# A conv-and-pooling decoder step: pair one by the plain products, and first chunks of weights that bring two thirds of x

## The chip, the cores and the metric

The kernel runs on one core of a Trainium2 chip. The metric is device time in microseconds of one execution. Of the core's engines, TensorE (PE in the profile, PEld for its weight loads) multiplies, VectorE (DVE) and ScalarE (ACT) do the elementwise work, SyncE (SP) issues the DMAs, and GpSimd (POOL) does nearly nothing.

## The reference

One layer of a decoder on 1024 prompt tokens and 32 sample tokens, 1056 in all, of 1024 channels, in float32:

```python
h    = x * rsqrt(mean(x * x) + eps) * norm_g
proj = h @ w_in                      # 1024 -> 3072: b, c, u, z_a, v, z_b, 512 columns each
cu   = c * u
y_a  = b * conv3(cu) * silu(z_a)     # 3 taps over time
y_b  = ((window mean of v) - v) @ pool_w * pool_scale * silu(z_b)   # windows 2, 4, 8, 16
x    = x + concat(y_a, y_b) @ w_out
y    = x * rsqrt(mean(x * x) + eps) * final_g
```

The last rows of cu and v go out too, as new states.

## The kernel before

**Tokens and channels.** Channels lie on the 128 partitions: 1024 channels of x are 8 chunks k. The 1056 tokens are three thirds n = 0, 1, 2 of 352 columns. `raw[n]` holds a third of x as loaded. The factor of the first RMS norm is one number per token, and it is applied after the projection: `R` holds it for all tokens, `R2` its square.

**Precision.** A float32 operand is split into an upper and a lower half of a shorter type (`split`, `split2`: ScalarE writes the upper half on L154, VectorE the lower half on L155). A product is three matmuls: upper by lower, lower by upper, upper by upper.

**Pairs.** The 24 blocks of 128 output columns of `w_in` are done two at a time, 12 pairs (`PAIRS`). Pair 0 (`project_first`) is done plain: for each third of tokens, 8 chunks x 3 products x 2 outputs = 48 matmuls, as the chunks of weights (`wfraw`, L108) and of x (`raw`, L105) arrive. The first six issues of weights each come with the same chunks of third 2; thirds 0 and 1 follow in halves.

**Strassen pairs.** Pairs 1 to 11 treat thirds 0 and 1 as two rows of blocks, and the lower and upper 4 chunks as two columns: A11, A12 (third 0) and A21, A22 (third 1). With sums S1 to S4 of blocks of x and differences T1 to T4 of blocks of weights, seven block products of 12 matmuls do for eight (function `block`, L229). Third 2 (`pl`) is done plain. That is 7 x 12 + 2 x 24 = 132 matmuls a pair. The weights of a pair p are loaded (`load_w`, into `wraw`, one buffer), scaled by the norm's gain on ScalarE (`gain_w`, eight operations, L203), differenced on VectorE (`make_t`, L208 to L210) and split into four units a (B11, B21), b (B12, B22), c (T1, T3), d (T2, T4) (`make_unit`). Units have five buffers (tag "wt").

**Places.** Tiles with one tag share a place, or as many as the tag has buffers; a new tile of a full tag gets a place when an old one is given back. S1, S2, S3, S4 have the tags "xa", "xc", "xb", "xd"; "xa", "xc" and "xd" held `raw[2]`, `raw[1]`, `raw[0]`, and "xb" held A21. Before their splits, the float32 sums S1f, S3f, S2f are formed in place in `raw[1]` and `raw[0]` (L500, L501, L507), S4f in two buffers of its own. PSUM has eight banks, which go round.

**Sums of squares.** Rows of tokens 0 to 639 are squared on ScalarE with an accumulator (`square_rows`, tiles t = 0 to 4). The other tokens are squared by channel (`squares_head`, `squares_last`), added up on VectorE (`sums_head`, `sums_last`) into `acc`, and summed over the partitions by 8 small matmuls (`sums_rest`, L276). `rows` makes the reciprocal roots, in two halves on a diagonal (L285 to L299), and `rows_out` spreads them over partitions with 6 matmuls (L306) into R and R2.

**The order.** The first part, to the end of pair 1, stands in `tc.manual_schedule` for TensorE, ScalarE, VectorE and GpSimd: these engines take its instructions in the order in which they are written. From pair 2 on only TensorE's order is written by hand; a planner places the rest by its own costs. DMAs are placed by the planner throughout. Pair 2 runs through `strassen` with two hooks: `rest` (sums_rest and rows) after its third block, T1, and `rows` (rows_out) after the plain product "l".

Of the kernel before, what the change touches and what calls it, by code (L numbers as in the profile page):

```python
# [7 lines left out]
F32 = mybir.dt.float32  # L8
# [5 lines left out]
P = 128  # L14
D = 1024
KD = D // P
# [46 lines left out]
def trunk(ctx, tc, xt, xres, xct, w_first, w_in, w_out, pool_w, par, fg, sconv, spool,  # L63
# [40 lines left out]
    def load_x(n, k, m):  # L104
        nc.sync.dma_start(raw[n][:, k:k + m, :], xt[:, n * KD + k:n * KD + k + m, :])  # L105

    for k, m in ((0, 1), (1, 1), (2, 1), (3, 1), (4, 2), (6, 2)):
        nc.sync.dma_start(wfraw[:, k:k + m, :], w_first[:, k:k + m, :])  # L108
        load_x(2, k, m)
    for n in (0, 1):  # L110
        for k in (0, 4):
            load_x(n, k, 4)

    wraw = {}

# [50 lines left out]
    def split_x(n, k, m):  # L166
        dst = blocks[n, k // KH]
        ks = slice(k % KH, k % KH + m)
        split2(dst[:, 0, ks], dst[:, 1, ks], raw[n][:, k:k + m])
# [11 lines left out]
    pm = {}  # L181
# [53 lines left out]
    def load_rows(t, xk):  # L235
        nc.sync.dma_start(xk, xres[t * P:(t + 1) * P])
        return xk
# [7 lines left out]
    def squares_head(acc):  # L245
        sh = tmp("sq_h")[:, :KD * REST].rearrange("p (k c) -> p k c", k=KD)
        nc.scalar.activation(sh, raw[1][:, :, TN - REST:], AF.Square)
        return sh
# [160 lines left out]
    def strassen(p, S1, S2, S3, S4, hooks):  # L409
        (q, j), (_, _) = PAIRS[p]  # L410
        if q == "v":
            left = vb[:, PM:]
            right = szb[j] = tmp(f"szb_{j}")
            scale = R
        elif q == "c":
            left, right = tmp(f"t_{j}"), tmp(f"um_{j}")
            scale = R2
        else:
            left, right = tmp(f"z_{j}"), tmp(f"y_{j}")
            scale = R  # L420
        n0, n1, n2 = cols

        def plain(i, name):
            pt = bank(name)[:, :TN]
            block(pt, p, ("B11", "B12")[i], pl[0], True, False)
            block(pt, p, ("B21", "B22")[i], pl[1], False, True)
            return pt

        a = bank(f"a_{p}")[:, :TN]
        s1 = snap(f"s1_{p}")  # L430
        block(a, p, "B11", A11, True, False)
        nc.scalar.copy(s1, a)
        b = bank(f"b_{p}")[:, :TN]
        block(b, p, "T2", S2, True, False)
        t1 = snap(f"t1_{p}")
        vt(t1, b, s1, op=ADD)  # L436
        c = bank(f"c_{p}")[:, :TN]
        block(c, p, "T1", S1, True, False)
        hooks.get("rest", lambda: None)()
        pL = plain(0, f"l_{p}")  # L440
        hooks.get("rows", lambda: None)()
        vt(left[:, n2], pL, scale[:, n2], op=MUL)
        block(a, p, "B21", A12, False, True)
        vt(left[:, n0], a, scale[:, n0], op=MUL)
        block(b, p, "T3", S3, False, False)
        t2 = snap(f"t2_{p}")
        vt(t2, b, s1, op=ADD)
        vt(right[:, n1], c, t2, op=ADD)
        hooks["early"]()
        pR = plain(1, f"r_{p}")  # L450
        if q == "v":
            vt(right[:, n2], pR, R[:, n2], op=MUL)
        elif q == "c":
            vt(up[:, 2 + 2 * TN:], pR, left[:, n2], op=MUL)
        else:
            nc.scalar.copy(right[:, n2], pR)
        hooks["middle"]()
        block(b, p, "T4", A22, False, True)
        vt(left[:, n1], b, s1, op=ADD)
        vt(left[:, n1], left[:, n1], scale[:, n1], op=MUL)  # L460
        block(c, p, "B22", S4, False, True)
        vt(right[:, n0], c, t1, op=ADD)
        hooks["late"]()

        if q == "v":
            after_v(j)
            vt(right[:, both], right[:, both], R[:, both], op=MUL)
            silu(right)
        elif q == "c":
            vt(up[:, 2:2 + 2 * TN], right[:, both], left[:, both], op=MUL)  # L470
            after_u(j)
        else:
            silu(left)
            vt(left, left, keep["yc"], op=MUL)
            vt(right, right, left, op=MUL)
            finish_mix(right, f"a_{j}")
# [5 lines left out]
    with tc.manual_schedule(engines={ET.PE, ET.Activation, ET.DVE, ET.Pool}):  # L482
        for k in range(KD):
            prep_w0(k)
            split_x(2, k, 1)
            project_first(2, k)
        nc.vector.tensor_copy(gain.rearrange("p (k o) -> p k o", o=1), wfraw[:, :, 2 * P:])
        load_w(1)
        nc.sync.dma_start(part, par)
        xk = [load_rows(t, q[:, :D]) for t, q in enumerate((R, R2, up[:, 2:]))]  # L490
        acc = tmp("acc")
        for n in (0, 1):
            for k in range(0, KD, 2):
                split_x(n, k, 2)
            for k in range(KD):
                project_first(n, k)
        sh = squares_head(acc)

        S1f, S3f, S2f = raw[1][:, KH:], raw[1][:, :KH], raw[0][:, :KH]
        vt(S1f, raw[1][:, :KH], raw[1][:, KH:], op=ADD)  # L500
        vt(S3f, raw[0][:, :KH], raw[1][:, :KH], op=ALU.subtract)  # L501
        gain_w(1)
        make_unit(1, "a")
        for i in range(2):
            nc.scalar.copy(heads[i][:, n2], pm[i, 2])
        sq = squares_last()
        vt(S2f, S1f, raw[0][:, :KH], op=ALU.subtract)  # L507
        make_t(1)
        make_unit(1, "b")
        load_w(2)  # L510
        S4f = [tp.tile([P, 2, TN], F32, tag="tmp", name=f"S4f_{h}") for h in range(2)]
        for h in range(2):
            vt(S4f[h], raw[0][:, KH + 2 * h:KH + 2 * h + 2], S2f[:, 2 * h:2 * h + 2], op=ALU.subtract)
        S1 = xtile("xa", "S1")
        split(S1, S1f)
        make_unit(1, "c")
        S3 = xtile("xb", "S3")
        split(S3, S3f)
        x34 = wp.tile([P, 2, D], F32, tag="wt", bufs=5, name="x34")
        xk += [load_rows(t, x34[:, t - 3]) for t in (3, 4)]  # L520
        for t in range(3):
            square_rows(t, xk[t])
        for n in (0, 1):
            for i in range(2):
                nc.scalar.copy(heads[i][:, cols[n]], pm[i, n])


        t_0, um = tmp("t_0"), tmp("um_0")

        def plain1(i):  # L530
            pt = bank(f"lr{i}_1")[:, :TN]
            block(pt, 1, ("B11", "B12")[i], pl[0], True, False)
            block(pt, 1, ("B21", "B22")[i], pl[1], False, True)
            return pt

        pL = plain1(0)
        pa, pb, pc = (bank(f"{q}_1")[:, :TN] for q in "abc")
        s1, t1, t2 = (snap(f"{q}_1") for q in ("s1", "t1", "t2"))
        block(pa, 1, "B11", A11, True, False)
        nc.scalar.copy(s1, pa)  # L540
        pR = plain1(1)
        block(pa, 1, "B21", A12, False, True)
        S2 = xtile("xc", "S2")
        split(S2, S2f)
        make_unit(1, "d")
        S4 = xtile("xd", "S4")
        for h in range(2):
            ks = slice(2 * h, 2 * h + 2)
            split2(S4[:, 0, ks], S4[:, 1, ks], S4f[h])
        nc.scalar.copy(t_0[:, n2], pL)  # L550
        block(pb, 1, "T2", S2, True, False)
        vt(t1, pb, s1, op=ADD)
        block(pc, 1, "T1", S1, True, False)
        sums = sums_last(acc, sq)
        gain_w(2)
        make_unit(2, "a")
        nc.scalar.copy(t_0[:, n0], pa)
        next(sums)
        block(pb, 1, "T3", S3, False, False)
        vt(t2, pb, s1, op=ADD)  # L560
        vt(um[:, n1], pc, t2, op=ADD)
        make_t(2)
        for t in (3, 4):
            square_rows(t, xk[t])
        vt(up[:, 2 + 2 * TN:], pR, t_0[:, n2], op=MUL)
        make_unit(2, "d")
        block(pb, 1, "T4", A22, False, True)
        vt(t_0[:, n1], pb, s1, op=ADD)
        block(pc, 1, "B22", S4, False, True)
        vt(um[:, n0], pc, t1, op=ADD)  # L570
        make_unit(2, "c")
        sums_head(acc, sh)
        for _ in sums:
            pass
        make_unit(2, "b")
        vt(up[:, 2:2 + 2 * TN], um[:, both], t_0[:, both], op=MUL)
    diag = []
    nc.sync.dma_start(scb[:, :, 0:2 * NB], sconv)
    nc.sync.dma_start(spb[:, :, 0:15 * NB], spool)

    def scale_heads():
# [7 lines left out]
        nc.sync.dma_start(pwraw, pool_w)  # L589
        split(pws, pwraw)  # L590
        after_v(0)

    def rest():
        sums_rest(acc)
        diag.extend(rows())

    def rows_2():
        rows_out(diag)

    def pair(p):  # L600
        nxt = p + 1 < NP
# [18 lines left out]

        hooks = {"early": early, "middle": middle, "late": late}
        if p == 2:
            hooks.update(rest=rest, rows=rows_2)
        strassen(p, S1, S2, S3, S4, hooks)
        if p == 3:
            pool_linear(0)
# [218 lines left out]
```

## Time and profile before

| | |
|---|---|
| median of 3 runs | 378.48 us (378.38 to 378.67) |
| profiled execution, own time | 378.59 us |
| its span | 376.8 us |
| granted TensorE clock, mean | 0.999 |
| TensorE busy with matmuls | 365.3 us, 2114 matmuls |
| VectorE busy | 275.3 us |
| ScalarE busy | 177.5 us |
| DMA | 41.68 MB, mean 111 GB/s |
| chain that ended last | PE 80%, ACT 8%, DVE 5%, DMA 4% |

The own time is that of the whole execution; the span is what the trace covers, and all times of rows count from its start. A row of the order in time gives start, duration, engine, line, operation, the tiles (written <- read), the count of merged instructions, and in brackets how long the engine had been idle before and what released it. Matmuls overlap: a merged row of n matmuls ends some 0.16 us after the step of the last one. DMA rows give the size and the time from issue to landing.

### The profile page before, as it was taken

The numbers are of one execution on the slowest core, as the hardware profiler recorded it, in microseconds if no ns is written. First come the engines' busy times: TensorE is split into PE (matmuls) and PEld (weight loads), VectorE is DVE, ScalarE is ACT, GpSimd is POOL, SyncE is SP. The second block draws the span as 40 slices with busy tenths as digits, with TensorE's granted clock in tenths as the row PEclk, the third lists the DMA queues.
The fourth block names the chain that finished last, engine by engine and source line by source line (L and its number), as shares of the span: only waits on it lengthen the run. The fifth ranks groups of instructions, "written<-read, shape, count | busy, mean of one in ns | idle before, by whom it ended". The sixth has DMA issues, their size and how long they took to land.

```text
span 376.8 us, 5274 instructions
## 1 busy us (share of the span) xinstructions
PE 365.3 (97%) x2114; PEld 349.2 (93%) x2114; DVE 275.3 (73%) x420; ACT 177.5 (47%) x310; POOL 1.4 (0%) x7
## 2 busy tenths in 40 slices
PE   7999999999999999999999999999999999999993
PEld 4999978999999999999999999999988889999883
DVE  4889689899999977578898557788279537222593
ACT  5899952985343454537353352731078224111212
POOL 0000000000000000000000000000000000000000
PEclk9999999999999999999999999999999999999999
DMA  7975002104031312103040320404549913000042
GB/s 198 413 282 202 14 0 87 54 2 151 18 113 58 117 54 90 82 2 111 2 169 0 110 90 16 153 6 164 236 128 354 417 71 150 20 1 2 0 181 111
DMA packets 13368, 41.68 MB, mean 111 GB/s; under 512 B 3744, under 2 KB 4896, under 8 KB 11936
## 3 DMA queue, kind: packets, MB, share of 16 engines
q1 hardware_dynamic: 13200, 41.02, 29.6%
q8 instruction: 16, 0.26, 0.3%
q10 hardware_dynamic: 144, 0.33, 0.2%
q14 instruction: 8, 0.07, 0.0%
HBM read 32.92 MB, written 8.42 MB: 110 GB/s over the span
## 4 chain that ended last, share of the span: by engine, by line
PE 80%; ACT 8%; DVE 5%; DMA 4%; issue 1%; SPq 1%; DVEq 0%; ACTq 0%
PE b L229 15%; PE po L675 15%; PE r L229 10%; PE a L229 10%; PE c L229 10%; PE pc L745 10%; PE l L229 9%; DMA raw<-in_xt_dram 4%; ACT wraw L203 2%; PE pp L383 2%; ACT S L154 1%; ACT diag L298 1%; ACT sq L259 1%; ACT R L240 1%; DVE A L155 0%
## 5 line engine op out<-in xcount | busy, mean ns | idle before, releaser
L675 PE MATMUL po<-wo,mix 128*128 128x512 f32 (+1 forms) x264 | 56.5, 374 | 0.0
L675 PEld LDWEIGHTS po<-wo,mix 128*128 128x128 f32 x264 | 46.2, 188 | 9.7 <-DVE mix L155 0.2
L229 PE MATMUL a<-A,wa 128*128 128x352 f32 x264 | 46.5, 324 | 0.2 <-DVE wa L155 0.2
L203 ACT ACTIVATE wraw<-wraw,gain 128x256 f32<-128x256 f32 x88 | 36.9, 497 | 18.0 <-DMA wraw<-in_w_in_dram 17.4
L229 PEld LDWEIGHTS a<-A,wa 128*128 128x128 f32 x264 | 43.3, 188 | 0.5 <-DVE wa L155 0.5
L229 PE MATMUL l<-pl,wa 128*128 128x352 f32 x240 | 40.5, 324 | 0.0
L229 PE MATMUL r<-pl,wb 128*128 128x352 f32 x240 | 40.4, 324 | 0.0
L229 PEld LDWEIGHTS r<-pl,wb 128*128 128x128 f32 x240 | 39.1, 188 | 0.0
L229 PEld LDWEIGHTS l<-pl,wa 128*128 128x128 f32 x240 | 39.1, 188 | 0.0
L745 PE MATMUL pc<-mix,wo 128*128 128x416 f32 x192 | 36.5, 351 | 0.0
L745 PEld LDWEIGHTS pc<-mix,wo 128*128 128x128 f32 x192 | 35.9, 188 | 0.5
L154 ACT ACTIVATE wd<-tw 128x1024 fp32r<-128x1024 f32 x11 | 11.7, 1064 | 30.5 <-DVE tw L210 26.8
L229 PE MATMUL b<-S,wd 128*128 128x352 f32 x132 | 23.8, 326 | 1.2 <-DVE wd L155 1.1
L229 PE MATMUL b<-A,wd 128*128 128x352 f32 x132 | 23.2, 324 | 0.5 <-DVE t L560 0.5
L229 PEld LDWEIGHTS b<-S,wd 128*128 128x128 f32 x132 | 21.6, 188 | 2.0 <-DVE wd L155 1.7
L229 PE MATMUL b<-S,wc 128*128 128x352 f32 x132 | 23.2, 324 | 0.0
L229 PE MATMUL c<-S,wc 128*128 128x352 f32 x132 | 23.2, 324 | 0.0
L229 PE MATMUL c<-S,wb 128*128 128x352 f32 x132 | 23.1, 324 | 0.0
L229 PEld LDWEIGHTS b<-A,wd 128*128 128x128 f32 x132 | 21.6, 188 | 0.8 <-DVE t L560 0.8
L229 PEld LDWEIGHTS b<-S,wc 128*128 128x128 f32 x132 | 21.6, 188 | 0.2 <-DVE t L436 0.2
L229 PEld LDWEIGHTS c<-S,wc 128*128 128x128 f32 x132 | 21.6, 188 | 0.1
L229 PEld LDWEIGHTS c<-S,wb 128*128 128x128 f32 x132 | 21.7, 188 | 0.0
(196 smaller groups left out, 523.4 us busy)
## 6 DMA issues: line engine op xcount, KB each, us to landing
wraw<-in_w_in_dram SPq DMA_DIRECT2D x11, 1024.0 KB, 4.6
woraw<-in_w_out_dram SPq DMA_DIRECT2D x8, 512.0 KB, 5.9
raw<-in_xt_dram SPq DMA_DIRECT2D x4, 704.0 KB, 9.0
zt<-in_xres_dram SPq DMA_DIRECT2D x5, 512.0 KB, 6.5
spill_b<-yb SPq DMA_DIRECT2D x4, 528.0 KB, 3.0
mixraw<-spill_b SPq DMA_DIRECT2D x4, 528.0 KB, 6.7
out_yt_dram<-zt SPq DMA_DIRECT2D x4, 512.0 KB, 2.6
zc<-in_xct_dram SPq DMA_DIRECT2D x4, 416.0 KB, 6.7
```

The source lines that it names most:

```text
L154: nc.scalar.activation(hi, src, AF.Copy)
L203: nc.scalar.activation(t, t, AF.Copy, scale=gain[:, k:k + 1])
L229: nc.tensor.matmul(pt, t[:, a, i, k * P:(k + 1) * P], x[:, b, k], start=first and s == 0, stop=last and s == len(seq) - 1, skip_group_chec ...
L240: nc.scalar.activation(xk, xk, AF.Square, accum_out=ss[:, t:t + 1])
L259: nc.scalar.activation(t, raw[2][:, k:min(k + 3, KD)], AF.Square)
L298: nc.scalar.activation(dh[:, t * P:t * P + m], ident[:, :m], AF.Copy, scale=rh[:, t:t + 1].bitcast(F32))
L383: nc.tensor.matmul(pt[:, :TN], pws[:, a, g, :], pooled[g][b][:, cols[n]], start=(s == 0), stop=(s == 2))
L675: nc.tensor.matmul(pt, mix[k][:, b, t * P:(t + 1) * P], wo[k][:, a, c], start=(k == 0 and s == 0), stop=(k == KD - 1 and s == 2))
L745: nc.tensor.matmul(pt, wo[k][:, a, d * P:(d + 1) * P], mix[k][:, b, T0:], start=(k == 0 and s == 0), stop=(k == KD - 1 and s == 2))
```

## The change

Three things are changed.

- *Loads and pair 0.* The first chunks of weights come in five issues (1, 1, 2, 2, 2 chunks) instead of six, and each comes with the same chunks of third 2 and of third 0. Pair 0 is done chunk by chunk for thirds 2 and 0, then for third 1.
- *Pair 1.* Instead of the Strassen form it is done plain: for each third (2, 0, 1) two products of 24 matmuls, with units a and b only, into six banks `pq`. S1 and S3 are formed and split ahead of these products in the text, S2 and S4 after the first two. The copies of pair 0's banks for thirds 2 and 0 come ahead of them. The scaling, the differences and units of pair 2, the squares and sums follow in a new order.
- *Row sums.* `sums_rest` and `rows` stand at the end of the first part, ahead of pair 2 and in the order written; `rows_out` stands where `sums_rest` stood. Unit b of pair 2 comes after `rows`.

```diff
-    for k, m in ((0, 1), (1, 1), (2, 1), (3, 1), (4, 2), (6, 2)):
+    for k, m in ((0, 1), (1, 1), (2, 2), (4, 2), (6, 2)):
         nc.sync.dma_start(wfraw[:, k:k + m, :], w_first[:, k:k + m, :])
         load_x(2, k, m)
-    for n in (0, 1):
-        for k in (0, 4):
-            load_x(n, k, 4)
+        load_x(0, k, m)
+    for k in (0, 4):
+        load_x(1, k, 4)
...
         block(c, p, "T1", S1, True, False)
-        hooks.get("rest", lambda: None)()
+        hooks.get("rows", lambda: None)()
         pL = plain(0, f"l_{p}")
-        hooks.get("rows", lambda: None)()
...
             prep_w0(k)
-            split_x(2, k, 1)
-            project_first(2, k)
+            for n in (2, 0):
+                split_x(n, k, 1)
+                project_first(n, k)
...
+        for k in range(0, KD, 2):
+            split_x(1, k, 2)
+        for k in range(KD):
+            project_first(1, k)
         sh = squares_head(acc)
+        gain_w(1)
+        make_unit(1, "a")
+        make_unit(1, "b")
+        load_w(2)
+        for n in (2, 0):
+            for i in range(2):
+                nc.scalar.copy(heads[i][:, cols[n]], pm[i, n])
+        sq = squares_last()
+        square_rows(2, xk[2])
...
         S1 = xtile("xa", "S1")
         split(S1, S1f)
-        make_unit(1, "c")
         S3 = xtile("xb", "S3")
         split(S3, S3f)
...
+        for i in range(2):
+            nc.scalar.copy(heads[i][:, n1], pm[i, 1])
+        t_0 = tmp("t_0")
+        pq = {}
+        for n in (2, 0, 1):
             for i in range(2):
+                pt = pq[i, n] = bank(f"pq_{i}_{n}")[:, :TN]
+                for h in range(2):
+                    block(pt, 1, (("B11", "B21"), ("B12", "B22"))[i][h], blocks[n, h], h == 0, h == 1)
+        nc.scalar.copy(t_0[:, n2], pq[0, 2])
+        vt(up[:, 2 + 2 * TN:], pq[1, 2], t_0[:, n2], op=MUL)
         S2 = xtile("xc", "S2")
         split(S2, S2f)
         S4 = xtile("xd", "S4")
         for h in range(2):
             ks = slice(2 * h, 2 * h + 2)
             split2(S4[:, 0, ks], S4[:, 1, ks], S4f[h])
+        gain_w(2)
+        make_t(2)
+        make_unit(2, "a")
+        make_unit(2, "d")
+        x34 = wp.tile([P, 2, D], F32, tag="wt", bufs=5, name="x34")
+        xk += [load_rows(t, x34[:, t - 3]) for t in (3, 4)]
+        for t in range(2):
+            square_rows(t, xk[t])
+        nc.scalar.copy(t_0[:, n0], pq[0, 0])
+        vt(up[:, 2:2 + TN], pq[1, 0], t_0[:, n0], op=MUL)
         sums = sums_last(acc, sq)
         next(sums)
+        for t in range(3, 5):
             square_rows(t, xk[t])
         make_unit(2, "c")
+        nc.scalar.copy(t_0[:, n1], pq[0, 1])
+        vt(up[:, 2 + TN:2 + 2 * TN], pq[1, 1], t_0[:, n1], op=MUL)
         sums_head(acc, sh)
         for _ in sums:
             pass
+        sums_rest(acc)
+        diag = rows()
         make_unit(2, "b")
...
         if p == 2:
-            hooks.update(rest=rest, rows=rows_2)
+            hooks["rows"] = lambda: rows_out(diag)
```

`blocks[n, h]` are the split thirds of x: A11, A12 for n = 0, A21, A22 for n = 1, `pl[0]`, `pl[1]` for n = 2.

More of the change, by code (lines that the diff above doesn't have):

```diff
@@ L491, in trunk @@
         acc = tmp("acc")
[L492 to L496, printed above, removed]
-        sh = squares_head(acc)
+        for k in range(0, KD, 2):
+            split_x(1, k, 2)
+        for k in range(KD):
+            project_first(1, k)
+        sh = squares_head(acc)
+        gain_w(1)
[7 more added lines that the diff above has]
+        square_rows(2, xk[2])
         S1f, S3f, S2f = raw[1][:, KH:], raw[1][:, :KH], raw[0][:, :KH]
@@ L501, in trunk @@
         vt(S3f, raw[0][:, :KH], raw[1][:, :KH], op=ALU.subtract)
[L502 to L506, printed above, removed]
         vt(S2f, S1f, raw[0][:, :KH], op=ALU.subtract)
-        make_t(1)
-        make_unit(1, "b")
-        load_w(2)
         S4f = [tp.tile([P, 2, TN], F32, tag="tmp", name=f"S4f_{h}") for h in range(2)]
@@ L515, in trunk @@
         split(S1, S1f)
-        make_unit(1, "c")
         S3 = xtile("xb", "S3")
         split(S3, S3f)
[L519 to L523, printed above, removed]
-            for i in range(2):
[L525 to L542, printed above, removed]
+        for i in range(2):
[3 more added lines that the diff above has]
+        for n in (2, 0, 1):
+            for i in range(2):
+                pt = pq[i, n] = bank(f"pq_{i}_{n}")[:, :TN]
[3 more added lines that the diff above has]
+        vt(up[:, 2 + 2 * TN:], pq[1, 2], t_0[:, n2], op=MUL)
         S2 = xtile("xc", "S2")
         split(S2, S2f)
-        make_unit(1, "d")
         S4 = xtile("xd", "S4")
@@ L549, in trunk @@
             split2(S4[:, 0, ks], S4[:, 1, ks], S4f[h])
[L550 to L553, printed above, removed]
+        gain_w(2)
[8 more added lines that the diff above has]
+        vt(up[:, 2:2 + TN], pq[1, 0], t_0[:, n0], op=MUL)
         sums = sums_last(acc, sq)
-        gain_w(2)
-        make_unit(2, "a")
-        nc.scalar.copy(t_0[:, n0], pa)
         next(sums)
[L559 to L563, printed above, removed]
-            square_rows(t, xk[t])
[L565 to L570, printed above, removed]
+        for t in range(3, 5):
+            square_rows(t, xk[t])
         make_unit(2, "c")
+        nc.scalar.copy(t_0[:, n1], pq[0, 1])
+        vt(up[:, 2 + TN:2 + 2 * TN], pq[1, 1], t_0[:, n1], op=MUL)
         sums_head(acc, sh)
@@ L574, in trunk @@
             pass
+        sums_rest(acc)
+        diag = rows()
         make_unit(2, "b")
-        vt(up[:, 2:2 + 2 * TN], um[:, both], t_0[:, both], op=MUL)
-    diag = []
     nc.sync.dma_start(scb[:, :, 0:2 * NB], sconv)
@@ L591, in scale_heads @@
         after_v(0)
[L593 to L598, printed above, removed]
     def pair(p):
```

## The prediction

> **What bounds the kernel now.** I read the totals first, then the matmul queue in order of time, then the two other engines around pair 1. The rows are: start us, us, engine, line, operation, tiles, count, and in brackets the idle time before it and what ended it.
>
> ```profile
> span 376.8 us, 5274 instructions
> ...
> PE 365.3 (97%) x2114; PEld 349.2 (93%) x2114; DVE 275.3 (73%) x420; ACT 177.5 (47%) x310; POOL 1.4 (0%) x7
> ```
>
> TensorE is busy for 97% of the span. Whatever makes it wait earlier adds to the end, and whatever takes a wait away from it is gained, but there are few waits to take.
>
> ```profile
> 4.23 1.32 PE L189 MATMUL pm<-pl,w 128*128 128x352 f32 x6
> 6.44 2.19 PE L189 MATMUL pm<-pl,w 128*128 128x352 f32 x12 [0.89 <-ACT pl L154]
> 9.63 1.23 PE L189 MATMUL pm<-pl,w 128*128 128x352 f32 x6 [1.00 <-ACT pl L154]
> 11.23 4.14 PE L189 MATMUL pm<-pl,w 128*128 128x352 f32 x24 [0.37 <-ACT pl L154]
> 15.21 15.65 PE L189 MATMUL pm<-A,w 128*128 128x352 f32 x96
> ...
> 30.70 4.04 PE L229 MATMUL lr<-pl,wa 128*128 128x352 f32 x24
> ```
>
> Pair 0 is 144 matmuls of 352 columns. The 96 of tokens 0 and 1 start at 15.21 and the next work starts at 30.70: 15.49 / 96 = 0.1614 us each. 144 of them are 23.24 us, the stretch from 4.23 to 30.70 is 26.47 us, so pair 0 holds 3.23 us of waiting, all of it while chunks of weights and of the last third of x arrive.
>
> ```profile
> 61.47 0.98 PE L276 MATMUL rest<-one,acc 128*128 128x1 f32 x8 [0.18 <-DVE acc L269]
> 62.38 4.16 PE L229 MATMUL l<-pl,wa 128*128 128x352 f32 x24
> 62.58 0.33 SPq L118 DMA_DIRECT2D wraw<-in_w_in_dram  x1
> 65.08 2.66 ACT L298 ACTIVATE diag<-ident,rh 128x128 fp32r<-128x128 f32 x9
> 66.38 1.21 PE L306 MATMUL pr<-diag,onesr 128*128 128x352 f32 x5
> 67.80 0.43 PE L306 MATMUL pr<-diag,onesr 128*128 128x352 f32 x1 [0.21 <-ACT diag L298]
> 68.06 2.10 PE L229 MATMUL a<-A,wa 128*128 128x352 f32 x12
> ```
>
> The row at 68.06 is block B21 of pair 2; after it the matmul queue is the same program in both kernels, and from here to the end TensorE is dense. So I compare the kernels at this point. Between 4.23 and 68.06 (63.83 us) lie 144 + 132 + 36 + 24 = 336 matmuls (54.23 us), 8 row-sum matmuls (62.38 - 61.47 = 0.91) and 6 of 352 columns (0.97): 56.1 us of work and 7.7 us of waits.
>
> **Part 1: the loads and pair 0.** The chunks k of x are split here on ScalarE:
>
> ```profile
> 3.68 0.50 ACT L154 ACTIVATE pl<-raw 128x352 fp32r<-128x352 f32 x1
> ...
> 9.08 0.50 ACT L154 ACTIVATE pl<-raw 128x352 fp32r<-128x352 f32 x1 [0.45 <-DMA raw<-in_xt_dram]
> ...
> 13.99 1.48 ACT L154 ACTIVATE A<-raw 128x704 fp32r<-128x704 f32 x2 [0.45 <-DMA raw<-in_xt_dram]
> ...
> wraw<-in_w_in_dram SPq DMA_DIRECT2D x11, 1024.0 KB, 4.6
> ```
>
> A chunk of weights is 128 x 257 x 4 = 132 KB, one of x 180 KB. From chunk 0 (3.68) to chunk 3 (9.08) 936 KB came in 5.40 us, 173 KB/us in single chunks; then 1.97 MB up to the first half of x0 (13.99) at 401 KB/us. With 492 KB a step, chunk 1 of the weights and both x land by 7.6 us, chunks 2-3 by 10.0, 4-5 by 12.5, 6-7 by 14.9. TensorE has 12 matmuls a chunk (1.94 us) instead of 6: (2,0) and (0,0) run 4.23 to 6.2, (2,1) from 7.0 and (0,1) to 9.0, (2,2) from 9.7 and from there without a break, since a pair of chunks takes 2.4 us to land and 3.9 to multiply. 72 + 48 matmuls from 9.7 (19.4 us) put the end of pair 0 at **29.1** against 30.70: 1.6 us gained. The bounds are no wait at all (27.5) and no gain (30.7). The one issue more on SP's queue (17 against 16) goes out before the data that it stands behind is through. The load of pair 1's weights now waits for the last split of x0, about 17.9 us; at 4.6 us it lands at 22.5, and its scaling (3.31), upper half (1.06) and lower half (1.22, rows below) end near 28.2, under pair 0.
>
> **Part 2: pair 1 on TensorE.** 6 x 24 = 144 matmuls for 132: +12 x 0.1614 = +1.94 us. Its weight units a and b are ready and its six banks were emptied before, so it runs 29.1 to 52.3 without a break.
>
> **Part 3: what now stands behind S3.** This part decides. Tile S3 lies in the place of A21 (both "xb"). In the kernel before, A21 is read last by pair 0. Now pair 1 reads it twice, last in the first half of its sixth product, (i, n) = (1, 1); the write of S3 has to wait for that. But the split of S3 stands early in the written order of ScalarE and VectorE, ahead of the splits of S2 and S4, of gain_w(2) and all weights of pair 2, and of the sums that the row-sum matmuls read. That such a wait holds up its whole queue shows here:
>
> ```profile
> 38.69 1.43 ACT L154 ACTIVATE S<-raw 128x1408 fp32r<-128x1408 f32 x1
> 40.15 1.62 DVE L155 TENSOR_TENSOR S<-raw,S 128x1408 fp32r<-128x1408 f32 x1 [1.61 <-ACT S L154]
> 41.80 1.47 ACT L154 ACTIVATE S<-S4f 128x704 fp32r<-128x704 f32 x2 [0.74 <-DVE S L155]
> 43.18 0.43 ACT L550 COPY t<-lr 128x352 f32<-128x352 f32 x1
> 43.52 3.31 ACT L203 ACTIVATE wraw<-wraw,gain 128x256 f32<-128x256 f32 x8
> 48.15 1.06 ACT L240 ACTIVATE x<-x 128x1024 f32<-128x1024 f32 x1
> 52.18 1.22 DVE L208 TENSOR_TENSOR tw<-wraw 128x1024 f32<-128x1024 f32 x1
> 54.16 0.69 DVE L210 TENSOR_TENSOR tw<-wraw,tw 128x512 f32<-128x512 f32 x1
> 54.88 1.06 ACT L154 ACTIVATE wd<-tw 128x1024 fp32r<-128x1024 f32 x1 [2.08 <-DVE tw L210]
> 55.84 1.04 ACT L154 ACTIVATE wc<-tw 128x1024 fp32r<-128x1024 f32 x1
> 57.98 1.22 DVE L155 TENSOR_TENSOR wc<-tw,wc 128x1024 fp32r<-128x1024 f32 x1
> 59.11 0.42 DVE L251 TENSOR_TENSOR sq_h<-sq_h 128x256 f32<-128x256 f32 x1
> 59.45 0.52 DVE L436 TENSOR_TENSOR t<-b,s 128x352 f32<-128x352 f32 x1
> ```
>
> At 41.80 the split of S4, whose source was long made, had waited 0.74 us until the split of S2 had read the last of x0, in whose place S4 lies; the copy of product "lr" (done at 34.74) stood behind it until 43.18. So places are waited for, in the order written.
>
> A21 is free after 132 matmuls of pair 1: 29.1 + 21.30 + the 0.16 by which a matmul's record outlasts its step = 50.6. From there, in the order written: S3's two halves 1.38 (as S2's, 1.43, less a little) + 1.62; S2's, which needs the place that S3 was read from, 1.43 + 1.62; S4's upper halves 1.47; gain_w(2) 3.31; make_t(2), three operations from 52.18 to 54.16 + 0.69 = 54.85, 2.67; upper half of wd until the next ScalarE start 0.96; two squares of 1.06, 2.12; copy of t_0 0.34; two more squares 2.12; wc's halves 1.04 + 1.22; the last product into up 0.52 (same shape as the row at 59.45); and from sums_head to the row-sum matmuls, 59.11 to 61.47 less the 0.43 that another pair's operation (59.45) took: 1.93. That is 23.75 us; some ten hand-overs of 0.03 and small overlaps leave **23.8**. VectorE's other work (wa, wd, first sums) fits beside it. The row sums, which TensorE has to do before pair 2, start at 74.4, where pair 1 ended at 52.3: a wait of 22 us. The bounds of this sum are 1 us either way (0.1 us on each of ten hand-overs, or as much overlap).
>
> **Part 4: the place of the row sums.** From their start to B21 of pair 2 now lie 0.91 + 36 matmuls (5.81) + 6 (0.97) + 24 (3.87) = 11.56 us; the row factors are done 6.3 us after their start (the row at 65.08 ends at 67.74, they start at 61.47), behind the 36 matmuls, so the 0.7 us of waits before 68.06 go. B21 starts at 74.4 + 11.56 = 86.0. Unit b of pair 2 now comes behind the row factors, at + 6.3 + 1.04 + 1.22 = 8.6 us from the row sums, and the load of pair 3's weights, which needs its place, moves from + 1.1 (62.58) to there, and lands near + 13.2. Scaling, make_t and two halves (3.31 + 2.67 + 1.06 + 1.22 = 8.3) then end near + 21.5 if little stands between; pair 3 wants that second unit at + 11.56 + 1.5 (part 5) + 84 matmuls (13.6) = 26.6. I count nothing for it; if rescaling the first pairs on VectorE gets in between for over 5 us, it costs 1 to 2 us.
>
> **Part 5: pace after the pause.**
>
> ```profile
> 0.77 3.81 PE L96 MATMUL warm<-const-bfloat16-1.0 128*128 128x512 bf16 x10 [0.77 <-PEq L838]
> ...
> L675 PE MATMUL po<-wo,mix 128*128 128x512 f32 x216 | 50.8, 394 | 0.0
> ```
>
> After no work at all, the first ten matmuls of 512 columns took 3.81 us, 0.38 each; in the last stage the same width took 50.8 / 216 = 0.235. So the start lost 3.81 - 2.35 = 1.5 us to a slow pace. Pauses up to 1.00 us (9.63) show none of it; no row has a pause of 22 us. The bounds are 0 and, if the slow stretch lasts twice as long, 3.0. A pause of 22 us is nearer to the idle start than to 1 us, so I take **1.5**.
> The Trainium skill, "TensorE: Matmul & The Clock Gate", Part 1 (The HAM clock gate), says that the array falls to half its clock after an idle window of about 3.4 us and needs about as long of work to come back; an estimate from that page is 1.7 us for one such pause, and by it the forecast would be 0.2 us higher. The granted clock of this trace reads 1.0 throughout, at the start too, so it doesn't show the gate.
>
> **The sum.** 86.0 + 1.5 - 68.06 = **+19.4 us**. In the parts: -1.6 (pair 0) + 1.9 (pair 1) + 22.1 (the wait) + 1.5 (pace) - 0.7 (row factors) and -3.8 for the waits that pair 1 and the start of pair 2 had before. The profiled execution took 378.59 us (0.1 above the median of the runs), 1.8 of it outside its span; I forecast **398.0**.
>
> **The rivals.**
> 1. *S3 doesn't wait* (it gets another place): for it speaks only that nothing in the profile of before shows a place whose old tile is read later in the text than the new one is written; against it that A21 is read and both have one place. Then VectorE's order sets the chain: wb's lower half ends near 29.4, S1f, S3f, S2f, S4f and two lower halves at 1.6 each give 39.2, and from S2 on the same 20.8 us: row sums at 60.0 against the end of pair 1 at 52.3. B21 at 71.6 to 73.1: **382 to 384**, slower still.
> 2. *Not slower: ready work passes the waiting split on ScalarE and VectorE.* If the planner puts gain_w(2), the units and the sums ahead of S3, only up's product and 1.9 us of sums stand between pair 1 and the row sums: 52.3 + 2.4 + 11.56 = 66.3, with no slow pace: **376.8**. It decides where gain_w(2) runs before 50 us. Against it: 41.80 above.
> 3. *No slow pace after the pause*: **396.5**; a slow stretch twice as long: 399.5. Both are inside the forecast's range.
> 4. *The loads bring nothing* or the larger first chunks arrive later: pair 0 ends at 30.7, **399.6**.
>
> **How the numbers follow.** Forecast with 3 and 4: 0.87, own range 394.5 to 401.8 (396.5 and 399.6 widened by the 1 us of the chain and 1 to 2 of part 4). Rival 1: 0.07. Rival 2: 0.04. Something unseen: 0.02. The first alone holds over 8 in 10. What a measurement tells from no change is about 0.2%, 0.76 us: faster 0.04, within 0.02, slower 0.94.
>
> **What would show it.** Right: a pause of some 20 us on TensorE between the last block of pair 1 and the row sums; ScalarE idle before S3's split, released by TensorE; gain_w(2) starting about 7.5 us after it; pair 0 ending near 29. Wrong: S3's split before the sixth product (rival 1), gain_w(2) before 50 us (rival 2), 352-column matmuls at 0.16 us right after the pause (part 5), a wait in pair 3 (part 4).

## The result

The changed kernel takes 399.98 us (median, 399.75 to 400.23) against 378.43 us before: a ratio of 1.0568, with a 95% interval of 1.055 to 1.0587. The forecast was 398.0 us, with a range of 394.5 to 401.8. The profiled execution took 399.92 us with a span of 398.1 us.

The page of the changed kernel: totals, and TensorE's busy tenths and granted clock in 40 slices of 10 us.

```profile
span 398.1 us, 5298 instructions
...
PE 367.9 (92%) x2126; PEld 354.1 (89%) x2126; DVE 269.3 (68%) x415; ACT 176.9 (44%) x312; POOL 1.4 (0%) x7
...
PE   8999930499999999999999999999999999999993
...
PEclk9999985599999999999999999999999999999998
```

The span grew by 21.3 us. TensorE's busy time rose by 2.6 us, 12 matmuls and some slow ones; the other 18.7 us are idle time: one hole of 21.9 us in the slices from 50 to 80 us, less some 3 us of short waits of the kernel before that are gone. In the same slices the granted clock falls to half. TensorE in order of time:

```profile
10.64 1.23 PE L189 MATMUL pm<-pl,w 128*128 128x352 f32 x6 [1.26 <-ACT pl L154]
...
21.38 8.87 PE L189 MATMUL pm<-A,w 128*128 128x352 f32 x54
30.09 4.05 PE L229 MATMUL pq<-pl,wa 128*128 128x352 f32 x24
...
49.49 4.04 PE L229 MATMUL pq<-A,wb 128*128 128x352 f32 x24
...
75.44 1.60 PE L276 MATMUL rest<-one,acc 128*128 128x1 f32 x8 [21.90 <-DVE acc L269]
76.97 3.89 PE L229 MATMUL a<-A,wa 128*128 128x352 f32 x12
...
89.46 2.10 PE L229 MATMUL a<-A,wa 128*128 128x352 f32 x12
```

The first row is third 2's chunk 2 in pair 0. Pair 0 ends at 30.09, pair 1 runs without a break to 53.5, and then TensorE waits 21.90 us for the sums that the row-sum matmuls read. Block B21 of pair 2 starts at 89.46, 21.4 us later than in the kernel before (68.06). From there to the end of the span it is 308.6 us, against 308.7 before: nothing is lost or won behind this point.

ScalarE and VectorE in the same stretch:

```profile
51.63 1.38 ACT L154 ACTIVATE S<-raw 128x1408 fp32r<-128x1408 f32 x1 [16.70 <-PE pq L229]
53.05 1.63 DVE L155 TENSOR_TENSOR S<-raw,S 128x1408 fp32r<-128x1408 f32 x1 [14.89 <-ACT S L154]
54.71 1.38 ACT L154 ACTIVATE S<-raw 128x1408 fp32r<-128x1408 f32 x1 [0.65 <-DVE S L155]
...
57.78 1.47 ACT L154 ACTIVATE S<-S4f 128x704 fp32r<-128x704 f32 x2 [1.69 <-DVE S L155]
59.15 3.28 ACT L203 ACTIVATE wraw<-wraw,gain 128x256 f32<-128x256 f32 x8
...
74.77 0.52 DVE L269 TENSOR_TENSOR acc<-acc,sq 128x352 f32<-128x352 f32 x1
```

The first row is the upper half of S3. ScalarE had been idle for 16.70 us and was released by TensorE's products of pair 1; VectorE had been idle for 14.89. Then S2's split, S4's, the scaling of pair 2's weights, its units and the sums follow one after the other: 23.81 us from the start of S3's split to the row sums. In the kernel before, most of this ran under pair 1's matmuls.

### The profile page after: what moved, and what is told of

The parts are those of the page before. It is cut to its first block, busy times and chain, and to the rows that moved or that the text cites. A ratio compares the mean times of both kernels' runs of the same rounds, so it can differ in the third digit from the quotient of the medians.

```text
span 398.1 us, 5298 instructions
## 1 busy us (share of the span) xinstructions
PE 367.9 (92%) x2126; PEld 354.1 (89%) x2126; DVE 269.3 (68%) x415; ACT 176.9 (44%) x312; POOL 1.4 (0%) x7
## 3 DMA queue, kind: packets, MB, share of 16 engines
q1 hardware_dynamic: 13344, 41.02, 28.2%
## 4 chain that ended last, share of the span: by engine, by line
PE 90%; ACT 4%; DVE 2%; DMA 2%; SPq 1%; issue 1%; DVEq 0%
PE b L229 15%; PE po L650 14%; PE a L229 10%; PE c L229 10%; PE l L229 10%; PE r L229 10%; PE pc L720 9%; PE pq L229 5%; PE pm L189 5%; DMA raw<-in_xt_dram 2%; PE pp L383 1%; ACT S L154 1%; DVE S L155 1%; ACT wraw L203 1%; ACT x L240 1%
## 5 line engine op out<-in xcount | busy, mean ns | idle before, releaser
L229 PE MATMUL a<-A,wa 128*128 128x352 f32 x240 | 43.8, 333 | 0.0
L229 PEld LDWEIGHTS a<-A,wa 128*128 128x128 f32 x240 | 40.8, 195 | 0.0
L208 DVE TENSOR_TENSOR tw<-wraw 128x1024 f32<-128x1024 f32 x10 | 12.2, 1225 | 15.4 <-ACT wraw L203 15.4
L276 PE MATMUL rest<-one,acc 128*128 128x1 f32 (+1 forms) x8 | 1.6, 313 | 21.9 <-DVE acc L269 21.9
L229 PE MATMUL b<-S,wd 128*128 128x352 f32 x120 | 21.1, 324 | 0.0
L229 PE MATMUL c<-S,wb 128*128 128x352 f32 x120 | 21.0, 324 | 0.0
L229 PE MATMUL c<-S,wc 128*128 128x352 f32 x120 | 21.0, 324 | 0.0
L229 PE MATMUL b<-S,wc 128*128 128x352 f32 x120 | 21.0, 324 | 0.0
L229 PE MATMUL b<-A,wd 128*128 128x352 f32 x120 | 21.0, 324 | 0.0
L229 PEld LDWEIGHTS b<-S,wd 128*128 128x128 f32 x120 | 19.9, 189 | 0.0
L229 PEld LDWEIGHTS c<-S,wc 128*128 128x128 f32 x120 | 19.7, 188 | 0.0
```

Of the source, the lines that this page charges most:

```text
L208: nc.vector.tensor_tensor(t[:, 0:2], w[:, 2:4], w[:, 0::2], op=ALU.subtract)
L229: nc.tensor.matmul(pt, t[:, a, i, k * P:(k + 1) * P], x[:, b, k], start=first and s == 0, stop=last and s == len(seq) - 1, skip_group_chec ...
L276: nc.tensor.matmul(pt[:m, i:i + 1], acc[:, i * P:i * P + m], one, start=True, stop=True)
```

## The experiments

Each run has the kernel before beside it on the same chip: 378.47 us in the first four runs, 378.66 in the next four, 378.75 in the last two.

### Without the late read of A21

```diff
-    block(pt, 1, (...)[i][h], blocks[n, h], h == 0, h == 1)
+    block(pt, 1, (...)[i][h], blocks[0 if h == 0 and n == 1 else n, h], h == 0, h == 1)
```

> The changed kernel, but the two products of pair 1 for third 1 read A11 where they read A21. The instructions and their sizes are the same; left out is the use of A21 in pair 1, so these columns of up are not the reference's. Nothing then reads the place of S3 after pair 0. Theory (the split of S3 waits for the last read of A21 and holds up two queues): S3's halves end near 39.7 behind S1's lower half (38.16), the chain from S2's split to the row sums takes the 20.7 us that it takes in the changed kernel (54.71 to 75.44), so the row sums start near 60.5 after a pause of 7 us, with 0 to 2.5 us of slow pace behind it: 382.5 to 385 us. Rival (the pause comes from the weights and sums of pair 2 being late in the text, whatever S3 waits for): no change, 400 us.

It took 385.33 us. TensorE in order of time:

```profile
60.20 1.60 PE L276 MATMUL rest<-one,acc 128*128 128x1 f32 x8 [6.99 <-DVE acc L269]
61.73 3.89 PE L229 MATMUL a<-A,wa 128*128 128x352 f32 x12
```

With the same instructions and one operand changed, the pause falls from 21.90 to 6.99 us and the row sums start at 60.20, as expected (60.5). The total is 0.3 us over the upper end of the theory's 382.5 to 385, for the slow pace behind the pause: 14.8 us from the row sums to B21. So 15 of the 22 us are the wait for A21's place. The other 7 are not: even with S3 free to go, the written order put the sums behind the weights of pair 2.

### Third 1 earlier in pair 1

```diff
-        for n in (2, 0, 1):
+        for n in (2, 1, 0):
```

> The changed kernel with one word of order: the products of pair 1 go over thirds 2, 1, 0 instead of 2, 0, 1. A21 is then read last 48 matmuls, 7.75 us, earlier; all else is the same. Theory (S3's place): the split of S3 starts at 43.9 instead of 51.63, the row sums at 67.7 instead of 75.4, the pause is 14 us instead of 22: 392.2 us. Rival (something at the end of pair 1 sets it): no change, 400 us.

392.16 us. TensorE at the row sums:

```profile
67.99 1.61 PE L276 MATMUL rest<-one,acc 128*128 128x1 f32 x8 [14.16 <-DVE acc L269]
```

S3's split starts at 44.17 (51.63 in the changed kernel), released by TensorE's products again. The last read of A21 comes 48 matmuls (7.75 us) earlier in pair 1, and the pause is shorter by 7.74 us: what releases the chain is that read, and nothing at the end of pair 1.

### The pause filled

```diff
+        pf = bank("fill")
+        for _ in range(95):
+            nc.tensor.matmul(pf, wz[:, 0:P], wz, start=True, stop=True)
         sums_rest(acc)
```

> The changed kernel with 95 further matmuls of constants, 512 columns each, between pair 1 and the row sums: they do nothing for the result and fill some 20.5 of the 21.9 us in which TensorE had nothing to do. Theory (the pause itself takes the granted clock to half, and that costs 2.5 us after it): the clock stays at 1.0 and the time falls by 2.5 us to 397.5. Rival (the first work after the pause is slow for another reason, its operands or its place in the program): no change, 400 us, or slower if the filling runs over.

Three executions took 398.75 to 399.11 us at a mean granted clock of 0.991 to 0.992, and one 397.01 us at 0.997: neither answer. TensorE in order of time, and two windows (start:end, length, busy time of PE, PEld, DVE, ACT and POOL, granted clock, DMA) of one of the longer ones:

```profile
74.86 0.95 PE L276 MATMUL rest<-one,acc 128*128 128x1 f32 x8 [1.09 <-DVE acc L269]
75.74 3.74 PE L229 MATMUL a<-A,wa 128*128 128x352 f32 x12
```

```profile
74.00:76.00 2.00, 1.15 (x9) 1.15 (x10) 0.68 (x2) 0.15 (x2) 0.00 (x0) 0.97 0.00 0
76.00:78.00 2.00, 2.00 (x8) 2.00 (x8) 1.23 (x7) 0.57 (x5) 0.00 (x0) 0.50 0.00 0
```

The pause was down to 1.09 us, and the clock held through the 21 us of filling, but it fell to 0.50 at 76 and came back near 79.3. Before, a pause of 1.00 us in pair 0 had shown no slow pace. So I made the filling longer:

```diff
-        for _ in range(95):
+        for _ in range(101):
```

> The changed kernel with 101 matmuls of constants instead of 95 in the pause, so that they end about where the sums are ready. With 95 the clock still fell, in the profiled execution from 76 to 79 us, after 1.1 us of pause and 0.9 us of one-column matmuls. Theory (the clock goes by the recent work of the array, and a short lull can be enough): with less lull it stays up, block B21 comes 11.6 us after the row sums (near 86.7), 397.1 us in all runs. Rival (constant operands don't count as work, so the clock falls whatever the filling's length): 398.9 us as with 95.

397.24 us, all four executions between 397.10 and 397.42.

```profile
74.79 0.88 PE L276 MATMUL rest<-one,acc 128*128 128x1 f32 x8
75.60 2.21 PE L229 MATMUL a<-A,wa 128*128 128x352 f32 x12
...
86.39 2.10 PE L229 MATMUL a<-A,wa 128*128 128x352 f32 x12
```

Without a lull, B21 comes 11.60 us after the row sums, where the changed kernel takes 14.02. So the slow pace behind the pause is worth 2.4 us, and it comes from the idleness and not from the work that follows it. The constant operands kept the clock up for 22 us. Why a lull of about 2 us (1.1 us of nothing, 0.9 us of one-column matmuls) was enough in three of four executions isn't shown, as only one of the four left a trace; the last section says what the traces show of the moments at which the clock changes.

### The loads alone

The diff of the loads and of pair 0's loops as in the change, and nothing else of it:

```diff
-    for k, m in ((0, 1), (1, 1), (2, 1), (3, 1), (4, 2), (6, 2)):
+    for k, m in ((0, 1), (1, 1), (2, 2), (4, 2), (6, 2)):
         nc.sync.dma_start(wfraw[:, k:k + m, :], w_first[:, k:k + m, :])
         load_x(2, k, m)
+        load_x(0, k, m)
...
```

> The kernel before with the loads and the order of pair 0 of the changed kernel, and nothing else of it: pair 1 by Strassen. Theory: TensorE ends pair 0 near 30.1 instead of 30.7, but the load of pair 1's weights is issued 4 us later and lands 1.4 us later (23.2 against 21.8 in the changed kernel), and ScalarE's chain from there to the units of pair 1 and 2 set the waits of pair 1 before: 378.4 to 379.9 us, same or slower. Rival (the loads are worth what TensorE gains in pair 0): 377.8 us.

379.80 us: a ratio to the kernel before of 1.0032, 95% interval 1.002 to 1.0043. TensorE and ScalarE in order of time:

```profile
22.98 3.31 ACT L203 ACTIVATE wraw<-wraw,gain 128x256 f32<-128x256 f32 x8 [2.08 <-DMA wraw<-in_w_in_dram]
...
29.60 4.04 PE L229 MATMUL lr<-pl,wa 128*128 128x352 f32 x24
...
69.26 2.09 PE L229 MATMUL a<-A,wa 128*128 128x352 f32 x12
```

TensorE ends pair 0 1.1 us earlier (30.70 before), and is at B21 1.2 us later (68.06 before). The second shift is that of pair 1's weights: their buffer is the one that held the first weights, which are now in use until third 0's last chunk is split, and their scaling starts at 22.98 instead of 21.80. Pair 1 by Strassen waits on ScalarE's chain, and that starts with this row; the two shifts, 1.18 and 1.20 us, agree, but no run moves this load alone.

### The row sums back in pair 2

```diff
         block(c, p, "T1", S1, True, False)
-        hooks.get("rows", lambda: None)()
+        hooks.get("rest", lambda: None)()
         pL = plain(0, f"l_{p}")
+        hooks.get("rows", lambda: None)()
...
-        sums_rest(acc)
-        diag = rows()
         make_unit(2, "b")
...
```

> The changed kernel with the row sums where they stood before the change: the 8 small matmuls and the row factors after the third block of pair 2, the 6 spreading matmuls after product l. S3's place stays as it is. Theory (S3's wait holds up the weights of pair 2 as well as the sums; the sums are only the later of the two): TensorE starts pair 2 when unit a is split, near 66.3 instead of 77.0, waits for unit c (72.9) before T1 and for the sums (75.3) as before, and then for the row factors, done 6.3 us later with 3.9 us of matmuls to cover them: block B21 near 82.7 instead of 89.5, 393.2 us. Rival (only the sums' place in TensorE's order makes the pause): pair 2 starts with no pause near 53, block B21 near 78 or before, 388 us or less.

393.68 us. TensorE in order of time:

```profile
62.92 0.66 PE L229 MATMUL a<-A,wa 128*128 128x352 f32 x1 [10.04 <-ACT wa L154]
65.67 3.54 PE L229 MATMUL a<-A,wa 128*128 128x352 f32 x11 [2.10 <-DVE wa L155]
...
73.78 2.04 PE L229 MATMUL c<-S,wc 128*128 128x352 f32 x11 [1.60 <-DVE wc L155]
76.12 0.98 PE L276 MATMUL rest<-one,acc 128*128 128x1 f32 x8 [0.31 <-DVE acc L269]
```

The pause is still there, now 10.04 + 2.10 us for unit a of pair 2, with smaller ones for unit c and the sums, and block B21 starts at 82.17 (82.7 expected). The place of the row sums added some 6 us; behind it stood the weights, held up by the same wait.

### S3 behind the sums

```diff
         S1 = xtile("xa", "S1")
         split(S1, S1f)
-        S3 = xtile("xb", "S3")
-        split(S3, S3f)
...
-        for n in (2, 0, 1):
+        for n in (2, 1, 0):
...
-        S2 = xtile("xc", "S2")
-        split(S2, S2f)
-        S4 = xtile("xd", "S4")
-        for h in range(2):
-            ks = slice(2 * h, 2 * h + 2)
-            split2(S4[:, 0, ks], S4[:, 1, ks], S4f[h])
         gain_w(2)
         make_t(2)
...
         xk += [load_rows(t, x34[:, t - 3]) for t in (3, 4)]
-        for t in range(2):
-            square_rows(t, xk[t])
-        nc.scalar.copy(t_0[:, n0], pq[0, 0])
-        vt(up[:, 2:2 + TN], pq[1, 0], t_0[:, n0], op=MUL)
         sums = sums_last(acc, sq)
         next(sums)
-        for t in range(3, 5):
+        sums_head(acc, sh)
+        for _ in sums:
+            pass
+        for t in (0, 1, 3, 4):
             square_rows(t, xk[t])
+        S3 = xtile("xb", "S3")
+        split(S3, S3f)
         make_unit(2, "c")
         nc.scalar.copy(t_0[:, n1], pq[0, 1])
         vt(up[:, 2 + TN:2 + 2 * TN], pq[1, 1], t_0[:, n1], op=MUL)
-        sums_head(acc, sh)
-        for _ in sums:
-            pass
+        S2 = xtile("xc", "S2")
+        split(S2, S2f)
         sums_rest(acc)
         diag = rows()
         make_unit(2, "b")
+        nc.scalar.copy(t_0[:, n0], pq[0, 0])
+        vt(up[:, 2:2 + TN], pq[1, 0], t_0[:, n0], op=MUL)
+        S4 = xtile("xd", "S4")
...
```

> The changed kernel with a new written order for the part behind pair 1's products: thirds 2, 1, 0; weights of pair 2 and the sums first, then S3's split, unit c, S2's split, the row factors, unit b, and S4's split last. The loads, pair 0, plain pair 1 and the row sums ahead of pair 2 stay as changed. Theory (what stood behind S3's wait was the whole loss): A21 is read last at 43.3, no queue waits for it; the sums are ready by 48.2, the second unit by 44.2, S2 by 53.2 against the end of pair 1 at 52.9: no pause, B21 at 52.9 + 11.6 = 64.5 to 65.5 against 68.06 in the kernel before: 374.9 to 376 us. Rival (pair 1 plain costs its 12 matmuls and something else in pair 2 or 3 waits, since the load of pair 3's weights comes late): 378 us or more.

376.42 us: 0.9936 of the kernel before, 95% interval 0.9916 to 0.9955. That is 0.4 us above the range expected, but it beats both kernels.

```profile
52.64 0.88 PE L276 MATMUL rest<-one,acc 128*128 128x1 f32 x8
...
61.66 4.14 PE L229 MATMUL l<-pl,wa 128*128 128x352 f32 x24 [0.86 <-ACT t L552]
65.64 2.10 PE L229 MATMUL a<-A,wa 128*128 128x352 f32 x12
```

No pause is left between pair 1 and the row sums. B21 is at 65.64, 2.4 us earlier than before, and 0.1 later than expected: product l waits for a bank that holds a product of pair 1, as I had put the copy behind unit b. Between its first 352-column matmul (4.64; 4.23 before) and B21 this kernel does 12 matmuls more than the kernel before, 1.9 us, and holds 3.1 us of waits and slow first matmuls where that one held 7.7. Plain pair 1 and the row sums ahead of pair 2 were not run apart, so how the gain divides between them isn't shown.

The same kernel with the loads and pair 0 of the kernel before:

> The kernel of the run with S3 behind the sums, but with the loads and the order of pair 0 of the kernel before: it tells what the loads are worth when pair 1 no longer waits for ScalarE. Theory: pair 0 ends 0.6 to 1.1 us later (30.7), and so does everything: 375.6 to 377 us, 0.6 to 1.1 above that run. Rival (the loads are worth nothing here either, as when they were changed alone): the same time as that run.

376.06 us: 0.9929 of the kernel before (0.9911 to 0.9947). It is not slower than the one with the new loads (the medians are 0.36 us apart and the ranges overlap); the rival holds. Pair 0 ends at 30.50 instead of 29.36, and B21 starts at 65.49, since l doesn't wait there.

### The bank freed early, with the new loads and the old

Against the two kernels of the section before:

```diff
         nc.scalar.copy(t_0[:, n1], pq[0, 1])
+        nc.scalar.copy(t_0[:, n0], pq[0, 0])
...
         make_unit(2, "b")
-        nc.scalar.copy(t_0[:, n0], pq[0, 0])
```

> The kernel of the run with S3 behind the sums, with one copy moved: the left product of third 0 leaves its bank on ScalarE right behind that of third 1, instead of behind unit b of pair 2. In that run product l of pair 2 had waited 0.86 us for this copy, as its bank is the same one. Theory (the 1.1 us that the new loads gain in pair 0 were lost at this bank): no wait at l, block B21 near 64.6 instead of 65.64: 375.4 us. Rival (ScalarE and VectorE set the pace there, and the next wait takes its place, for instance the row factors): 376.4 us.

> The same copy moved in the kernel with the loads of before. There l didn't wait. Theory: no change from the run without the move, 376.1 us, and the difference to the other kernel of this call is what the loads are worth, 0.7 us. Rival: both the same time, the loads are worth nothing.

With the new loads 376.20 us (376.11 to 376.54), 0.9931 of the kernel before (0.9917 to 0.9945); with the old ones 375.90 (375.62 to 376.98), 0.9928 (0.9912 to 0.9943). The first is 0.8 us above what was expected, and the old loads are not 0.7 us slower: both rivals hold. TensorE with the new loads:

```profile
64.91 2.10 PE L229 MATMUL a<-A,wa 128*128 128x352 f32 x12
...
78.49 0.32 PE L229 MATMUL b<-S,wd 128*128 128x352 f32 x1
79.33 2.05 PE L229 MATMUL b<-S,wd 128*128 128x352 f32 x11 [0.52 <-DVE wd L155]
```

The wait at l is gone. Of the 0.8 us that pair 0 ends earlier (29.75 against 30.55), 0.3 are lost at the 6 spreading matmuls, and B21 starts 0.5 us before that with the old loads (65.42). The rest is lost at the second unit of pair 3: its lower half ends at 79.28 here and at 78.99 with the old loads, where TensorE comes just in time for it. The loads are worth nothing here either: where TensorE gets there earlier, the next thing that it needs isn't ready.

## Why the prediction was right

The forecast named the mechanism, and the runs show it: the split of S3 waited for the last read of A21 (taking that read away, or moving it, moved the pause by 14.9 and 7.7 us), both elementwise engines stood behind it in the order written, and the chain behind it set the row sums.

- **Part 1, the loads.** Of the wrong size. Pair 0 was to end at 29.1 and ended at 30.09 in the profiled execution; other runs with the same loads and pair 0 show 29.4 to 30.4. I had let TensorE run without a break from 9.7; it waited 1.26 us for chunk 2 and went on at 10.64. ScalarE's splits of third 0's chunks 1 and 2 show the landings:

```profile
7.60 0.50 ACT L154 ACTIVATE A<-raw 128x352 fp32r<-128x352 f32 x1 [1.06 <-DMA raw<-in_xt_dram]
...
10.98 0.50 ACT L154 ACTIVATE A<-raw 128x352 fp32r<-128x352 f32 x1 [0.39 <-DMA raw<-in_xt_dram]
```

  Chunk 1 was in at 7.60, as forecast. The step that failed is the rate at which the next issues, chunks 2 and 3, land: 984 KB in 3.38 us, 291 KB/us, where I had taken the 401 KB/us of later loads. The weights of pair 1 I had through at 28.2, counting one unit; both were through at 30.03, and the second isn't read before 33.97. That the loads *alone* would be slower was not in the prediction; it had the later load of pair 1's weights, but hidden under pair 0, which holds for plain pair 1 only.
- **Part 2, pair 1.** Right: 144 matmuls without a break, 30.09 to 53.5.
- **Part 3, what stands behind S3.** Right: 23.8 us forecast, 23.81 measured; the pause 22 forecast and 21.90 measured. It started 1.0 us later, as pair 0 ended later. That the sum agrees to 0.01 us is partly luck: single terms are off by up to 0.2 us (from sums_head to the row sums 2.15 for 1.93) and cancel.
- **Part 4, the place of the row sums.** Right: 11.56 us from there to B21 forecast, 11.60 in the run in which the clock stayed up; the 6 spreading matmuls no longer wait for the row factors, and pair 3 doesn't wait either, for which I had counted nothing. That may hang on the late start: in the kernel with the bank freed early, with B21 at 64.91 instead of 89.46 and another order written, pair 3 does wait.
- **Part 5, the pace.** The mechanism was right, the size was not: 1.5 us forecast, 2.4 measured (14.02 - 11.60). The windows of the changed kernel show why (same columns as above):

```profile
53.50:57.00 3.50, 0.04 (x1) 0.00 (x0) 2.49 (x3) 1.94 (x3) 0.00 (x0) 0.98 0.00 0
57.00:60.00 3.00, 0.00 (x0) 0.00 (x0) 2.14 (x3) 2.22 (x5) 0.00 (x0) 0.50 0.00 0
...
79.00:80.70 1.70, 1.70 (x8) 1.70 (x7) 1.52 (x8) 1.61 (x7) 0.00 (x0) 0.50 0.00 0
80.70:83.00 2.30, 2.30 (x16) 2.30 (x15) 0.68 (x4) 2.30 (x7) 0.00 (x0) 0.98 0.03 7
```

  The clock was at half from about 56.9, 3.4 us into the pause, to 80.8, 5.3 us after the row sums began. I had taken 3.8 us, the length of the slow start. The Trainium skill, "TensorE: Matmul & The Clock Gate", Part 1, gives at least one idle window of about 3.4 us for the fall and at least one busy window of about 3.4 us for the return. The fall 3.4 us into the pause agrees with this (with the row sums back in pair 2 it came sooner, 2.5 us after the last matmul); the return took 5.3 us from the row sums, 3.8 us from the first 352-column matmul, and the 1.7 us that I had estimated from that page were too few as well.
- **The sum.** +19.4 us forecast and +21.4 measured at B21: 1.0 us from pair 0 and 0.9 from the pace, and the rest is rounding. Both errors go the same way, so none hides the other.
- **The rivals.** Rival 1 (S3 doesn't wait) was worked out as 382 to 384 us; the kernel in which A21 is not read late took 385.33, more by the longer slow pace. Rival 2 (ready work passes the waiting split) didn't happen: gain_w(2) ran at 59.15, behind S3's, S2's and S4's splits, and not before 50. What it would have given, 376.8, is close to what the kernel with a like order written by hand takes, 376.42, though that one also does third 1 before third 0.

## What to carry to other kernels

When a tile gets the place of another, look for the last reader of the old one in the whole text, not only up to the line of the new one: an engine whose order is written by hand stands still there, with all that is written behind it. Work that nothing waits for soon (here S3 and S4) belongs behind work that TensorE will need next. An earlier arrival at one step is worth something only if the inputs of the next step come earlier too: the same loads gained 0.8 to 1.1 us in pair 0 and lost it at different places in three kernels.

## What the runs showed of the hardware

The granted clock fell to 0.50 in the pauses of 22, 14, 10 and 7 us, 2.5 to 3.8 us after the last matmul, and came back 5.3 us (changed kernel), 6.2 us (third 1 earlier) and 7.0 us (without the late read) after the row sums had started. These times look like no rule, but the traces show one: within each trace, any two changes of the granted clock lie a whole multiple of 3.413 us apart.

| run | falls at | back at | half pace | from there to the next fall, near the end |
|---|---|---|---|---|
| changed kernel | 56.89 | 80.78 | 23.89 = 7 x 3.413 | 314.02 = 92 x 3.413 |
| third 1 earlier | 57.12 | 74.19 | 17.07 = 5 x 3.413 | 314.03 = 92 x 3.413 |
| row sums back in pair 2 | 55.37 | 69.02 | 13.65 = 4 x 3.413 | 320.85 = 94 x 3.413 |
| without the late read | 56.99 | 67.23 | 10.24 = 3 x 3.413 | 314.03 = 92 x 3.413 |
| pause filled, 95 matmuls | 75.88 | 79.29 | 3.41 = 1 x 3.413 | 314.03 = 92 x 3.413 |

So the clock was changed only at the steps of a grid of 3.413 us. In all five it came back at the end of the first interval of this grid that was full (to within 0.1 us) of 352-column matmuls, 3.3 to 5.5 us after these had begun. The cost of a pause therefore hangs also on where it falls in the grid: 2.4 us in the changed kernel and 3.2 without the late read (14.78 us from the row sums to B21 instead of 11.60), where 1.5 was forecast.

A lull of 2 us behind 21 us of constant matmuls made the clock fall too, in three executions of four; in the traced one the interval before the fall held 1.3 us of constant matmuls, 1.1 us of nothing and 0.9 us of one-column matmuls. That the fourth was spared because its lull lay otherwise in the grid is likely, but not shown. The pauses of up to 1.47 us in pair 0 left no slow pace (six matmuls behind them took 1.23 us). And at the start of the kernel the granted clock of the profile reads 1.00 while ten matmuls of 512 columns take 3.8 to 4.4 us, where 101 such matmuls took 22.26 us in the filled pause; so a granted clock of 1.0 there doesn't mean full pace.
